# A bidirectional encoder layer on one core: PSUM banks kept through the Fourier stages, V in quarters, tables two tiles ahead, and h^T copies of odd blocks only

## The chip, the cores and the metric

The kernel runs on one core of a Trainium2 chip. The metric is the device time of one execution in microseconds, median of several runs. The core has TensorE (PE; its weight loads are listed as PEld), VectorE (DVE), ScalarE (ACT), GpSimd (POOL) and SyncE (SP), which here issues most of the DMAs. Work is in SBUF (128 partitions), matmuls add up in PSUM (eight banks), and the inputs and large intermediates lie in DRAM.

## The reference

16 learned meta tokens are put ahead of 2048 tokens of width 1024, and the stream (T = 2064 positions) passes a LayerNorm. One projection then feeds two mixers:

```python
def fourier_mix(u):
    ug = u.astype(jnp.float32).reshape(Bn, L, N_FOURIER_GROUPS, FOURIER_GROUP_DIM)
    y = jnp.fft.fft2(ug, axes=(1, 3), norm="ortho").real
...
proj = jnp.einsum("bld,de->ble", x, w_in)
u_f, qkv, beta_l, decay_l, z, gates = jnp.split(proj, cuts, axis=-1)
y_a = jnp.einsum("blf,fd->bld", fourier_mix(u_f), w_fourier_proj)
y_b = jnp.einsum("blf,fd->bld", gated_delta_branch(qkv, ...), w_delta_proj)
mix = jnp.einsum("bld,de->ble", gate_a * y_a + gate_b * y_b, w_out)
x = layer_norm(DEEPNORM_ALPHA * x + mix, ln1_g, ln1_b)
ff = jnp.einsum("blf,fd->bld", jnp.square(jax.nn.relu(jnp.einsum("bld,df->blf", x, w_up))), w_down)
```

The Fourier mixer takes the real part of a DFT over the 2064 positions and the 128 channels of each of four groups. The delta branch (short convolution on q, k, v; four heads; forward and backward scans), the gates, the output projection, the MLP and two more LayerNorms follow; the diff touches none of them. Inputs and output are fp32.

## The kernel before, in words

**Number format.** An fp32 operand is held as two fp16 halves, high and low. `split` (L56) makes them: ScalarE writes the high half, VectorE the rest. `mm3` (L91) then issues three matmuls for each block of 128 (high by high, high by low, low by high; L95 to L97).

**LayerNorm and channel DFT** (`phase_ln0_fourier`, L143). `ln(t)` loads a tile of 128 tokens (`x0`, three buffers), takes the statistics on VectorE with the root on GpSimd, normalises into `h`, stores `h` for later (`z_sc`), transposes it by TensorE into banks `ps0`, scales it on ScalarE into `ht` (four buffers), and splits it on VectorE into the fp16 halves `hb` (16 tiles of 128 tokens, four blocks of 512) and `hm` for the meta tokens. Each half of `ht` is also stored in fp32 to DRAM (`htd`, L194). `wprime(q)` (L203) multiplies the Fourier columns of the projection by the channel DFT table once, for eight q, and `uprime` (L196) multiplies h^T by that: `uT`, four row groups m of 128 channels by 2064 positions in fp32. Its eight weight loads `wt` are issued on ScalarE's queue (L165).

**Folding** (L232). The DFT over positions is made shorter by symmetry: for each m, positions are added to or subtracted from their mirror image twice (`f`, `f2`), transposed, and split into `V` (one tile of 128 x 2 halves x 2 parities x 5 blocks x 512 channels). All four m stand behind the last `uprime` in the program.

**Position DFT** (`phase_dft`, L255). Eight tables (sine or cosine s, parity, half of the frequencies c), each 0.5 MB in fp16, are loaded into `dtab` (three buffers), and for each two or three products of 15 matmuls are made into a bank `psf` and split into `yf` (m = 0, 1) or `y6`, the four channels in the middle of the groups. `y6` goes by three DMAs into `yf64`.

**ya** (`phase_ya`, L325). For each of eight column blocks d the weights are prepared (`prep_wf`, one d ahead), and in three steps of 344 positions the products for the even and the odd part are made, added and subtracted on VectorE into `ya`, and stored.

**Side work** (`h_ops`, L636). The later projections use a seven-product scheme (Strassen) and need sums of blocks of h^T: for each of two pairs of blocks and four column groups j, four blocks are loaded back from `htd` into `raw`, and T1 to T4 are made by four subtractions and split. `h_ops` is a generator: the stages resume it with `next(side)`, four times ahead of the DFT, once after each of its 16 large products, once after each of the 24 steps of ya; what is left runs at the end (`drive(side)`). Its instructions on ScalarE and VectorE are kept in program order.

**qkv** (`phase_qkv`, L713). It begins with `prep_in(0, ...)` (L810), which loads two blocks of the weights, makes four sums and seven split operands `wu` (eight buffers `tile16`) and stores these for the second pass. Then groups of seven products follow.

**What sets the order.** The program is written in this sequence, and a planner, which models each engine's time, gives each engine a fixed order: an instruction that is ready and stands earlier in the program goes first. Loads can so be issued long before their place, as soon as their buffer is free. On the chip each engine and each DMA queue keeps its order, and a waiting instruction holds back all behind it. A buffer pool that is opened later lies over the memory of pools that were closed, and its tiles wait until the tiles they lie on are no longer used: `winp` (`raw`, `sum`, `wu`), `yfp` (`yf`, `yf64`, `wfs`) and `dft` (`dtab`) lie over the tiles of the LayerNorm stage. The PSUM pools are separate for each stage: five banks `psf` and three `ps0` in LayerNorm, four `psf` in the DFT and ya.

Of the kernel before, what the change touches and what calls it, by code (L numbers as in the profile page):

```python
# [142 lines left out]
def phase_ln0_fourier(k, pr, vp):  # L143
# [8 lines left out]
    k.htd = k.dram.tile([4, 2, 4, P, 512], F32, name="htd")  # L152
    V = vp.tile([P, 2, 2, NQT, 512], F16, name="V")
    with k.pool("fft") as fp, k.pool("ln0") as lp, k.pool("ln0s") as sp, \
            k.pool("ln0p", bufs=3, space=PSUM) as tp, k.pool("fftp", bufs=5, space=PSUM) as pp:
# [8 lines left out]
        for q in range(KT):  # L164
            nc.scalar.dma_start(out=wt[:, q], in_=i["w_inf_t"][q])  # L165
# [3 lines left out]
        def ln(t):  # L169
# [9 lines left out]
            for q in range(2):  # L179
# [13 lines left out]
                if t > 0:  # L193
                    nc.sync.dma_start(out=k.htd[(t - 1) // 4, q, (t - 1) % 4].rearrange("p (j c) -> p j c", c=P), in_=ht)  # L194
# [8 lines left out]
        def wprime(q):  # L203
            wth = fp.tile([P, 2, 4, P], F16, name="wth", bufs=3)
            split(k, wth[:, 0], wth[:, 1], wt[:, q], S_W)
            ps = pp.tile([P, 4, P], F32, name="psf")
            for g in range(4):
                mm3(k, ps[:, g], lambda _: wth[:, 0, g], lambda _: wth[:, 1, g],
                    lambda _: ctab[:, 0], lambda _: ctab[:, 1], 1)
            pv = ps.rearrange("p g (s j) -> p g s j", s=2)  # L210
            dv = [wp[:, e, q].rearrange("p (s g j) -> p g s j", s=2, g=4) for e in range(2)]
            for e in range(2):
                split(k, dv[0][:, :, e], dv[1][:, :, e], pv[:, :, e], 1.0 / S_TAB)

        ln(0)
        ln(1)
        for q in range(KT):
            wprime(q)
        ln(2)
        for t in range(1, 5):  # L220
            if t == 1:
                uprime(range(4), 0, MT)
            uprime(range(4), MT + (t - 1) * P, P)
            for j in ((3,), (4,), (5, 6), (7, 8))[t - 1]:
                ln(j)
        for b in range(1, 4):
            for m in range(4):
                uprime([m], *HBLK[b])
                if b < 3:
                    ln(4 * b + 5 + m)  # L230
        for m in range(4):
# [7 lines left out]
            for par in range(2):  # L239
# [4 lines left out]
                for q in range(2):  # L244
# [5 lines left out]
                    o = [V[:r, e, par, 4 * q:4 * q + nb, m * P:(m + 1) * P] for e in range(2)]  # L250
                    split(k, o[0], o[1], ps[:r, :nb], 1.0)
    return V


def phase_dft(k, V, yp, fp, pp, side, h):  # L255

# [4 lines left out]
    y6 = fp.tile([4, 2, NK + 1], F16, name="y6")  # L261
    yf64 = yp.tile([68, NK + 1], F16, name="yf64")
    nc.gpsimd.memset(yf64, 0.0)
    for _ in range(4):
        next(side, None)
    wf0 = prep_wf(k, yp, 0, 1, h)
    for s in range(2):
        for par in range(2):
            for c in range(2):
                k0, kn = c * KW, min(KW, NQ - par - c * KW)  # L270
                tb = fp.tile([P, NQT, 2, KW], F16, name="dtab", bufs=3)
                src = i["dft_tab"][s, par, c]
                nc.sync.dma_start(out=tb[:, :4], in_=src[:4 * P].rearrange("(n p) e k -> p n e k", p=P))
                nc.sync.dma_start(out=tb[:rl, 4], in_=src[4 * P:])
                for m in range(3 - s):
                    M = P if m < 2 else 4
                    cols = slice((2 * s + m) * P, (2 * s + m + 1) * P) if m < 2 else slice(256, 512, 64)
                    ps = pp.tile([P, 512], F32, name="psf")
                    for n in range(NQT):
# [7 lines left out]
                    if m < 2:  # L287
                        next(side, None)
# [666 lines left out]
def drive(g):  # L955
    for _ in g:
        pass
# [924 lines left out]
```

## Time and profile before

| What | Value |
|---|---|
| median of 3 runs | 2747.83 us (2745.06 to 2750.65) |
| profiled execution | 2750.99 us, its span 2749.2 us, mean granted clock 0.982 |
| TensorE busy | 2614.9 us, 95% of the span |
| VectorE busy | 1944.4 us, 71% |
| ScalarE busy | 1210.4 us, 44% |
| DMA | 521.81 MB, mean 190 GB/s |
| first 280 us (stages that the diff touches) | about a tenth of the span |

A time in the trace is counted from the first instruction. "PE" rows are matmuls, which overlap, so that the distance from one start to the next says more than a duration. An arrow in brackets names who ended the idle time ahead of an instruction. The granted clock is TensorE's, 1.00 being full speed.

### The profile page before, as it was taken

How to read it: one execution, taken by the hardware profiler on the slowest of the kernel's cores; microseconds unless marked ns; L12 is line 12 of the kernel's file. 1: busy time of each engine (PE TensorE's matmuls, PEld its weight loads, DVE VectorE, ACT ScalarE, POOL GpSimd, SP SyncE). 2: the span in 40 equal slices, each digit the busy share in tenths (PEclk: the TensorE clock that was granted, in tenths of full speed). 3: DMA queues.
4: the chain of work that ended last, by engine and by line, in shares of the span. 5: the costliest groups of instructions: out<-in, count | busy, mean ns of one | idle time of the engine just before them, and what ended most of it. 6: DMA issues, size and time to landing. Idle time of an engine off the chain costs nothing.

```text
span 2749.2 us, 42069 instructions
## 1 busy us (share of the span) xinstructions
PE 2614.9 (95%) x15087; PEld 1393.4 (51%) x15087; DVE 1944.4 (71%) x3785; ACT 1210.4 (44%) x2772; POOL 401.6 (15%) x559
## 2 busy tenths in 40 slices
PE   6987999999899989999999999999999999999997
PEld 6454555455554449986444444444444444444443
DVE  7558897888878316687968688888888655545556
ACT  5434565555563325685222454444553422222232
POOL 1000131121010001263156500000001300000003
PEclk9988999999999999999999999999999999999999
DMA  7568666589898757774822674444446733333311
GB/s 263 190 204 289 208 222 209 165 285 305 283 322 287 268 193 227 219 243 143 282 86 76 191 284 141 144 152 161 169 169 242 244 100 104 100 104 100 103 43 73
DMA packets 325850, 521.81 MB, mean 190 GB/s; under 512 B 84220, under 2 KB 136396, under 8 KB 321672
## 3 DMA queue, kind: packets, MB, share of 16 engines
q1 hardware_dynamic: 320712, 512.88, 56.5%
q10 hardware_dynamic: 4928, 6.24, 0.7%
q8 instruction: 118, 1.93, 0.3%
q14 instruction: 92, 0.75, 0.1%
HBM read 311.30 MB, written 207.69 MB: 189 GB/s over the span
## 4 chain that ended last, share of the span: by engine, by line
PE 67%; DVE 15%; DMA 7%; issue 3%; ACT 3%; POOL 3%; SPq 1%; DVEq 0%; POOLq 0%; ACTq 0%
PE mm L95 17%; PE mm L97 17%; PE mm L96 17%; DVE wu L59 2%; PE psf L95 1%; PE psf L97 1%; PE psf L96 1%; PE psc L1216 1%; DVE hid L498 1%; PE psc L1241 1%; DVE hb L59 1%; PE psc L1233 1%; PE psc L1253 1%; PE psc L1224 1%; DVE acc L1578 1%
## 5 line engine op out<-in xcount | busy, mean ns | idle before, releaser
L95 PE MATMUL mm<-hb,wu 128*128 128x512 f16 x1280 | 487.8, 381 | 12.4 <-ACT wu L58 7.4
L96 PE MATMUL mm<-hb,wu 128*128 128x512 f16 x1280 | 487.5, 381 | 0.0
L97 PE MATMUL mm<-hb,wu 128*128 128x512 f16 x1280 | 487.3, 381 | 0.0
L1578 DVE TENSOR_TENSOR acc<-acc,mm 128x512 f32<-128x512 f32 x420 | 285.5, 683 | 150.2 <-PE mm L97 149.4
L95 PE MATMUL mm<-wdn,hid 128*128 128x512 f16 x904 | 342.2, 379 | 13.4 <-DVE acc L1578 13.3
L96 PE MATMUL mm<-wdn,hid 128*128 128x512 f16 x904 | 342.6, 379 | 0.0
L97 PE MATMUL mm<-wdn,hid 128*128 128x512 f16 x904 | 342.5, 379 | 0.2 <-DVE hid L498 0.2
L95 PEld LDWEIGHTS <-wu 128*128 128x128 f16 x1900 | 185.2, 98 | 220.1 <-ACT wu L58 11.8
L96 PEld LDWEIGHTS <-wu 128*128 128x128 f16 x1900 | 184.9, 98 | 218.2 <-issue 18.7
L97 PEld LDWEIGHTS <-wu 128*128 128x128 f16 x1900 | 184.6, 98 | 213.8 <-issue 5.4
L95 PE MATMUL mm<-ht,wu 128*128 128x512 f16 x512 | 196.7, 384 | 8.0 <-DVE c L606 4.2
L96 PE MATMUL mm<-ht,wu 128*128 128x512 f16 x512 | 196.6, 384 | 0.0
L97 PE MATMUL mm<-ht,wu 128*128 128x512 f16 x512 | 196.0, 383 | 0.0
L498 DVE TENSOR_TENSOR hid<-c,hid 128x512 f16<-128x512 f32 x158 | 107.3, 686 | 124.9 <-ACT hid L497 124.7
L66 POOL TENSOR_SCALAR ln_rs<-ln_mv 128x1 f32<-128x1 f32 (+1 forms) x49 | 13.7, 280 | 1192.4 <-DVE ln_mv L76 1182.5
L497 ACT CAST hid<-c 128x512 f16<-128x512 f32 x158 | 95.7, 614 | 183.7 <-PE mm L97 155.1
L96 PEld LDWEIGHTS <-hid 128*128 128x128 f16 x904 | 88.4, 98 | 122.7 <-issue 19.7
L751 DVE SCALAR_TENSOR_TENSOR conv<-rawc,cw,conv 128x512 f32<-128x512 f32 x192 | 135.0, 741 | 14.9 <-ACT conv L749 14.5
L58 ACT ACTIVATE wdn<-raw 128x512 f16<-128x512 f32 x78 | 46.4, 622 | 222.6 <-PE mm L97 187.3
L97 PEld LDWEIGHTS <-hid 128*128 128x128 f16 x904 | 88.3, 98 | 108.2 <-DVE hid L498 2.2
L95 PEld LDWEIGHTS <-hid 128*128 128x128 f16 x904 | 88.4, 98 | 107.2 <-ACT hid L497 1.2
L58 ACT ACTIVATE wu<-raw 128x512 f16<-128x512 f32 x145 | 88.0, 622 | 77.5 <-PE mm L97 45.2
(385 smaller groups left out, 4982.3 us busy)
## 6 DMA issues: line engine op xcount, KB each, us to landing
wu<-op SPq DMA_DIRECT2D x245, 256.0 KB
op<-wu SPq DMA_DIRECT2D x203, 256.0 KB
wdn<-op SPq DMA_DIRECT2D x112, 256.0 KB
op<-wdn SPq DMA_DIRECT2D x98, 256.0 KB
kq<-kqd SPq DMA_DIRECT2D x46, 512.0 KB
raw<-in_w_down SPq DMA_DIRECT2D x36, 512.0 KB
raw<-in_w_qz SPq DMA_DIRECT2D x32, 512.0 KB
gt<-c SPq DMA_DIRECT2D x64, 256.0 KB
```

The source lines that it names most:

```text
L58: nc.scalar.activation(out=hi, in_=src, func=AF.Copy, scale=scale)
L59: nc.vector.scalar_tensor_tensor(out=lo, in0=src, scalar=scale, in1=hi, op0=ALU.mult, op1=ALU.subtract)
L95: mm(ps, lhsT=whi(q), rhs=xhi(q), start=first and q == 0, stop=False, skip_group_check=skip)
L96: mm(ps, lhsT=whi(q), rhs=xlo(q), start=False, stop=False, skip_group_check=skip)
L97: mm(ps, lhsT=wlo(q), rhs=xhi(q), start=False, stop=last and q == nk - 1, skip_group_check=skip)
L497: k.nc.scalar.copy(t[:, 0], src)
L498: k.nc.vector.tensor_tensor(out=t[:, 1], in0=src, in1=t[:, 0], op=ALU.subtract)
L751: nc.vector.scalar_tensor_tensor(out=s, in0=src[:, j:j + m], scalar=cw[:, c, j:j + 1], in1=s, op0=ALU.mult, op1=ALU.add)
L1216: nc.tensor.matmul(ps[:, h], lhsT=kq[:, h, 0], rhs=S[:, h], start=True, stop=True)
L1224: nc.tensor.matmul(psq[:, h], lhsT=kq[:, h, 1], rhs=S[:, h], start=True, stop=True)
L1233: nc.tensor.matmul(psv[:, h], lhsT=T_[:, h], rhs=R[:, h], start=True, stop=True)
L1578: nc.vector.tensor_tensor(out=c, in0=c, in1=ps, op=ALU.add)
```

## The change

- The `psf` pool (five banks) is opened once, around LayerNorm, DFT and ya.
- `V` becomes four tiles, one for each m, and a small fifth one (`V6`) with the middle channels, filled by ScalarE copies. `fold(0)` and `fold(1)` stand behind the last `uprime` of m = 2 and m = 3, `fold(2)` and `fold(3)` at the end.
- The tables get two buffers in pool `dft` and one, `dtab0`, in the pool of V, which lies over nothing; each table is loaded two to three steps ahead. The third product of a step (middle channels) comes after the next step's two, and its results go straight into `yf64`.
- `h_ops` is resumed twice after each DFT product and no more ahead of them. `prep_wf` is two d ahead.
- `htd` is stored for the second and fourth block of h^T only; `h_ops` takes the others from the fp16 halves, with one VectorE instruction more for each of two sums.
- The first qkv operands are made by the same side generator, behind `h_ops`; the call at the start of `phase_qkv` goes.
- `wprime` writes its bank in the order of the result, so that one split does for two; seven of eight `wt` loads move to SyncE's queue.

```diff
-    k.htd = k.dram.tile([4, 2, 4, P, 512], F32, name="htd")
-    V = vp.tile([P, 2, 2, NQT, 512], F16, name="V")
+    k.htd = k.dram.tile([2, 2, 4, P, 512], F32, name="htd")
+    V = [vp.tile([P, 2, 2, NQT, P], F16, name="V%d" % m) for m in range(4)]
+    V.append(vp.tile([P, 2, 2, NQT, 4], F16, name="V6"))
...
-                if t > 0:
+                if t > 0 and (t - 1) // 4 % 2:
...
-            ps = pp.tile([P, 4, P], F32, name="psf")
+            ps = pp.tile([P, 512], F32, name="psf")
+            pv = ps.rearrange("p (s g j) -> p g s j", s=2, g=4)
...
-            for e in range(2):
-                split(k, dv[0][:, :, e], dv[1][:, :, e], pv[:, :, e], 1.0 / S_TAB)
+            split(k, wp[:, 0, q], wp[:, 1, q], ps, 1.0 / S_TAB)
...
+                    o = V[m][:r, :, par, 4 * q:4 * q + nb]
+                    split(k, o[:, 0], o[:, 1], ps[:r, :nb], 1.0)
+                    if m > 1:
+                        for e in range(2):
+                            nc.scalar.copy(V[4][:r, e, par, 4 * q:4 * q + nb, 2 * m - 4:2 * m - 2], o[:, e, :, ::64])
+
+        ln(0)
+        for q in range(1, 4):
+            nc.sync.dma_start(out=wt[:, q], in_=i["w_inf_t"][q])
+        ln(1)
+        for q in range(4, KT):
+            nc.sync.dma_start(out=wt[:, q], in_=i["w_inf_t"][q])
...
+                elif m > 1:
+                    fold(m - 2)
+        fold(2)
+        fold(3)
...
+    def load():
+        if len(tabs) < len(steps):
+            t = steps[len(tabs)]
+            tb = tabs[t] = (fp.tile([P, NQT, 2, KW], F16, name="dtab", bufs=2) if len(tabs) % 3 else
+                            vp.tile([P, NQT, 2, KW], F16, name="dtab0"))
...
+            split(k, yf64[:4, ks], yf64[32:36, ks], ps[:M, :kn], ysc)
+            nc.scalar.copy(yf64[64:68, ks], yf64[:4, ks])
+        if m < 2:
+            next(side, None)
+            next(side, None)
+
+    for _ in range(3):
+        load()
+    third = []
+    for t in steps:
+        s = t[0]
+        load()
+        for m in range(2):
+            prod(t, m)
+        if t == steps[0]:
+            wf0 = [prep_wf(k, yp, d, 1, h) for d in range(2)]
+        if third:
+            prod(third.pop(), 2)
         if s == 0:
+            third.append(t)
...
-        if d + 1 < KT:
-            ops.append(prep_wf(k, mp, d + 1, 2))
+        if d + 2 < KT:
+            ops.append(prep_wf(k, mp, d + 2, 2))
...
-            r = [h.raw() for _ in range(2)]
+            r = h.raw()
             for q in range(2):
-                for e in range(2):
-                    nc.sync.dma_start(out=r[q][:, 512 * e:512 * e + 512], in_=k.htd[2 * p + e, q, j])
+                nc.sync.dma_start(out=r[:, 512 * q:512 * q + 512], in_=k.htd[p, q, j])
...
-            add(t1, b12, b11)
+            add(z(t1), z(b12), b11[:, 0, :, c])
+            add(z(t1), z(t1), b11[:, 1, :, c])
...
-            add(t4, b21, t2)
+            add(z(t4), b21[:, 0, :, c], z(t2))
+            add(z(t4), z(t4), b21[:, 1, :, c], ALU.add)
...
-        h.prep_in(0, [col(f) for f in G[0]])
...
+                pp = cy.enter_context(k.pool("psfp", bufs=5, space=PSUM))
...
-                    side = h_ops(k, h)
-                    pp = cy.enter_context(k.pool("dftp", bufs=4, space=PSUM))
+                    side = chain(h_ops(k, h), h.prep_steps(0, (4, 0)))
```

`chain` runs one generator after the other. `prep_steps`, `w_steps` and `left_steps` are `prep_in`, `prep_w` and `left` with pauses between the operands.

147 lines of the change are left out of this document (76 added, 71 removed).

## The prediction

> **What bounds the kernel now.** I read the page first, then the stretches of the stages that the diff touches, then TensorE's and SyncE's rows in order of time, and last VectorE's groups. The page says that TensorE bounds the program as a whole:
>
> ```profile
> span 2749.2 us, 42069 instructions
> PE 2614.9 (95%) x15087; PEld 1393.4 (51%) x15087; DVE 1944.4 (71%) x3785; ACT 1210.4 (44%) x2772; POOL 401.6 (15%) x559
> ```
>
> All edits lie before the qkv stage, so the share of the whole says little. The stretches by stage (time, then each engine's busy time, the granted clock, DMA):
>
> ```profile
> core 0: us, PE busy (x) PEld busy (x) DVE busy (x) ACT busy (x) POOL busy (x), PEclk, DMA share, GB/s
> 30.00:142.00 112.00, 102.17 (x885) 65.00 (x882) 68.21 (x138) 50.68 (x137) 13.11 (x33) 0.97 0.56 205
> 142.00:160.00 18.00, 9.42 (x46) 6.04 (x45) 15.43 (x34) 7.75 (x20) 0.96 (x1) 0.63 0.42 124
> 160.00:199.00 39.00, 38.97 (x298) 25.57 (x297) 20.91 (x40) 14.35 (x32) 0.00 (x0) 0.95 0.80 261
> 199.00:264.00 65.00, 52.71 (x312) 31.20 (x310) 52.78 (x110) 26.12 (x55) 0.34 (x1) 0.92 0.86 284
> 220.00:240.00 20.00, 14.76 (x93) 8.73 (x92) 19.79 (x41) 9.09 (x19) 0.00 (x0) 0.97 0.88 322
> 264.00:278.00 14.00, 5.07 (x26) 1.93 (x26) 7.92 (x19) 4.70 (x8) 0.00 (x0) 0.70 0.90 308
> ```
>
> They are: LayerNorm with the channel products (to 142), folding and transposes into V (to 160), the position DFT (to 199), ya (to 264), the entry of qkv (to 278). TensorE is full in the DFT, where VectorE is only half used (20.91 of 39). In ya VectorE is used to 81% (52.78 of 65), for a while to 99% (19.79 of 20), and TensorE waits. Around the two seams TensorE stands still and its clock falls. Its rows there (start, duration, in brackets the idle time and its releaser):
>
> ```profile
> 63.92 0.66 PE L182 MATMUL ps<-ident,h 128*128 128x128 f32 x4 [4.52 <-ACT ht L189]
> ...
> 142.02 1.15 PE L249 MATMUL ps<-ident,x 128*128 128x128 f32 x9
> ...
> 159.18 0.38 PE L95 MATMUL psf<-dtab,V 128*128 128x259 f16 x1 [4.47 <-DMA dtab<-in_dft_tab]
> 159.35 0.42 PE L96 MATMUL psf<-dtab,V 128*128 128x259 f16 x1
> 159.56 0.43 PE L97 MATMUL psf<-dtab,V 128*128 128x259 f16 x1
> ...
> 164.17 0.27 PE L95 MATMUL psf<-dtab,V 128*128 128x259 f16 x1
> 164.28 0.28 PE L96 MATMUL psf<-dtab,V 128*128 128x259 f16 x1
> ...
> 261.45 0.31 PE L95 MATMUL psf<-yf,wpm 128*128 128x344 f16 x1
> 261.60 0.31 PE L96 MATMUL psf<-yf,wpm 128*128 128x344 f16 x1
> ...
> 269.91 0.61 PE L95 MATMUL mm<-hb,wu 128*128 128x512 f16 x1 [7.42 <-ACT wu L58]
> 270.31 0.63 PE L96 MATMUL mm<-hb,wu 128*128 128x512 f16 x1
> ...
> 277.48 0.61 PE L95 MATMUL mm<-ht,wu 128*128 128x512 f16 x1 [3.02 <-ACT wu L58]
> ```
>
> The first seam runs from 142.02 to 159.18 us, the second from the end of ya (269.91 - 7.42 = 262.5) until qkv flows after 277.48. Matmuls follow each other at 0.11 us (259 columns) and 0.15 us (344) when warm, and at twice that right behind the idle time (159.35 to 159.56).
>
> SyncE's queue at the first seam shows what the tables wait for:
>
> ```profile
> 144.17 1.74 SPq L689 DMA_DIRECT2D raw<-htd  x4
> 153.32 1.42 SPq L298 DMA_DIRECT2D wfs<-in_wf_parts  x3
> 154.78 0.47 SPq L273 DMA_DIRECT2D dtab<-in_dft_tab  x1
> ```
>
> The raw blocks go out when uT is last read, wfs when the last fold is over, and the table behind them.
>
> **LayerNorm stage.** Half of the htd stores go, and seven of the eight wt loads move from ScalarE's queue to SyncE's, three ahead of the first full x tile. The wp split becomes one pair of instructions instead of two.
>
> VectorE's wait for x up to 290 us, and the transfers from 30 to 100 us:
>
> ```profile
> DVE ln_st L74 <- DMA x<-in_x: 9.3, 6, 2.0
> ...
> DMA packets 6450, 19.59 MB, mean 280 GB/s; under 512 B 704, under 2 KB 704, under 8 KB 6080
> ...
> htd<-ht SPq DMA_DIRECT2D x23, 256.0 KB
> ```
>
> VectorE's two groups of the folded weights, and the first of their loads:
>
> ```profile
> L59 DVE SCALAR_TENSOR_TENSOR wp<-psf,wp 128x256 f16<-128x256 f32 x16 | 6.1, 419 | 0.7 <-ACT wp L58 0.4
> L59 DVE SCALAR_TENSOR_TENSOR wth<-wt,wth 128x512 f16<-128x512 f32 x8 | 5.3, 684 | 0.2
> ...
> 1.74 0.94 ACTq L165 DMA_DIRECT2D wt<-in_w_inf_t  x2
> ```
>
> VectorE waits 9.3 us for x. From 30 to 100 us the engines move 19.59 MB at 280 GB/s, and 23 htd stores of 0.26 MB are 6 MB of it; half of them is 3 MB, or 10.7 us of transfer, at the place where x is late. The most that can come back is TensorE's idle time from 30 to 142, 112 - 102.2 = 9.8 us, and the slow clock, 3% of 112 = 3.4: 13 us. The wp split saves 6.1 - 5.3 = 0.8 us of VectorE. The other end: a wt load takes 0.94 / 2 = 0.47 us to issue, and seven of them put 3.3 us in front of x on SyncE: +3 us. I take -7, a little over the middle, because x is the wait that ends last there and its competitor is halved.
>
> The Trainium skill says in "DMA: Bandwidth & Descriptors", section "Issuing engines are not separate DMA queues", that all issuing engines feed the same 16 DMA engines and another issuer saves only the issuing time. It speaks against the move to SyncE: by it the transfers gain nothing and only the +3 us end is left of that edit; the -7 would be -4.
>
> **VectorE from the last fold to the end of the first qkv operands.** The groups of VectorE from 142.8 to 264 (count, busy us, mean ns):
>
> ```profile
> L59 DVE SCALAR_TENSOR_TENSOR V<-ps,V 128x512 f16<-128x512 f32 (+1 forms) x16 | 6.9, 478 | 1.6 <-ACT V L58 1.5
> L683 DVE TENSOR_TENSOR sum<-raw 128x512 f32<-128x512 f32 x15 | 10.2, 680 | 0.0
> L683 DVE TENSOR_TENSOR sum<-raw,sum 128x512 f32<-128x512 f32 x14 | 9.6, 686 | 0.2
> L59 DVE SCALAR_TENSOR_TENSOR yf<-psf,yf 128x259 f16<-128x259 f32 (+2 forms) x16 | 7.2, 450 | 13.7 <-ACT yf L58 13.7
> ```
>
> And three of its rows in order of time:
>
> ```profile
> 142.85 1.29 DVE L238 SCALAR_TENSOR_TENSOR h<-uT,sgn 128x1031 f32<-128x1031 f32 x1 [3.67 <-ACT uT L201]
> ...
> 266.79 0.68 DVE L683 TENSOR_TENSOR sum<-raw 128x512 f32<-128x512 f32 x1
> 267.39 0.68 DVE L673 TENSOR_TENSOR wu<-sum,wu 128x512 f16<-128x512 f32 x1
> ```
>
> The first is the last fold's beginning. The others give the pitch: such instructions take 0.68 us but follow each other at 0.60. I count in that pitch, as the stretches do.
> - Now: 15.43 + 20.91 + 52.78 = 89.1 us in the stretches, and behind 264 what is left of h_ops, eight instructions of which the two sum rows lack three of 32 adds, at 0.60, 4.8 us: 94.
> - Away: the V splits of block 0 move ahead of 142, a quarter of 6.9: -1.7.
> - New: each of the eight blocks of h_ops rebuilds b11 and b21 from two halves with two further adds: 16 x 0.60 = 9.6. The trace has no add of this mix (fp32 and fp16 in, fp32 out). Below, the plain fp16 cast of equal size at 0.42, above, the fp32 adds here; I take the upper end, since these are adds with an fp32 output. The lower would save 3 us.
> - Moved: the first qkv operands, four adds and seven splits, 11 x 0.60 = 6.6, from behind 276 into ya.
>
> Sum: 93.9 - 1.7 + 9.6 + 6.6 = 108.4 us. TensorE has 300 matmuls at 0.11 and 312 at 0.15 (the counts in the DFT and ya stretches) and some 30 transposes at 0.13: 33 + 46 + 4 = 83. **VectorE becomes the bound of this stretch.** That is the center of the forecast: the seams of TensorE vanish only as far as VectorE lets them.
>
> How well can it be used? The side work is called twice after each DFT product (32 calls) and once after each ya step (24): 56, which is what eight blocks of six calls, one call more and seven of operand work need; today there are 44, and what is left of them stands in the second seam. So the 18 us that VectorE idles in the DFT are filled. Bounds: 81% as in ya now, 98.9% as from 220 to 240. I take 88%, nearer to the first, because the splits still alternate with ScalarE (13.7 us of waits in the yf row). 108.4 / 0.88 = 123; from 142.85 to 266. TensorE can start qkv four instructions earlier, 4 x 0.60 = 2.4 us, at 263, with the last operands still being split.
>
> And now? The first product of qkv has 12 matmuls, done by 277.48, where the second begins cold again: 0.40 us apart (269.91 to 270.31), of which half is the warm rate. Taking as many cold matmuls behind 277.48 as the first product has, the 12 x 0.2 us lost there cancel the 12 x 0.2 us of work already done: as if qkv had begun warm at 277.5. Gain 277.5 - 263 = 14, less one for a clock that will not be full at the entry: **-13**, with bounds 277.5 - (142.9 + 108.4 / 0.989 - 2.4) = 27 and 277.5 - (142.9 + 108.4 / 0.81 - 2.4) = 3.
>
> **At nothing.** The tables two tiles ahead and the kept banks: their 4.47 us wait lies in the seam already counted, covered by VectorE's folds until about 153; without that cover it is 4.5 us. Three transfers y6 to yf64 become splits at the same price and four copies on ScalarE, idle for half of the DFT (14.35 of 39). Sixteen tiny V6 copies, at most 0.3 us each, fall on ScalarE in the folds (7.75 of 18). The second wf set made early: the same instructions, moved. The seven stores of the operands move into ya, where half of the htd loads fall away.
>
> **Sum.** -7 - 13 = -20 against the profiled execution's 2750.99: 2731. The median of the runs is 3.2 lower, 2747.83, so **2728 us**. The stages behind 278 should move forward as they are: their order does not depend on a fixed time.
>
> **Rivals.**
> - *VectorE full, LayerNorm's waits all gone* (-27 - 13 = -40: 2708). For it: 19.79 of 20. Against: a stretch of 110 us with four engines in turns.
> - *VectorE no better used than in ya today* (-3, and LayerNorm -1: 2744). For it: the adds are new work on the engine that becomes the bound. Against: the wf operands, which caused part of ya's waits, come one step earlier.
> - *The tables do not come early*, because their two other buffers lie over tiles of LayerNorm that the folds use to the end: wfs goes out at 153.3 for that reason. Then the second table lands at 158, TensorE has had two products of the DFT, and VectorE lost some yf splits that it makes up for: +3, 2731.
> - *Slower: TensorE's clock.* TensorE would have 83 us of work in 120 and be idle in between for VectorE. Behind idle time the rows show half rate. If the granted clock stays low over the whole stretch, TensorE takes over as the bound once its mean is below 83 / 120 = 0.69. At half rate the work takes 166 us, to 309 instead of 277.5: +31 - 7 = +24, on the scale of the median 2772. For it: 0.63 and 0.70 at the seams. Against: 0.97 from 220 to 240, where TensorE is busy 14.76 of 20, much as it would be.
>
> The Trainium skill, "TensorE: Matmul & The Clock Gate", section "Part 1: The HAM clock gate (the "warmup" mystery)", has this as a rule: an idle window of about 3.4 us halves the clock, and as much busy time frees it. The trace agrees with the halving (0.22 against 0.11 us); the waits of the stretch from 220 to 240 stayed below what brings it about.
>
> **How the numbers follow.** Forecast 56% (2716 to 2737: LayerNorm -10 to -3, VectorE used to 95 or 85%), full use 12%, poor use 17%, late tables 9%, clock 6%. What a measurement here can tell from no change is 0.2%, some 5.5 us, so from 2742.3 to 2753.3 is the same. Faster: nearly all of the forecast, full use, late tables and a little of poor use: 0.79. Same: most of poor use: 0.12. Slower: clock and the tail of poor use: 0.09. The range leaves out the clock and the far half of full use: 2709 to 2747.
>
> **What would show it.** VectorE busy above 85% between the last fold and qkv, with TensorE idle in small pieces and a clock above 0.9; the first DFT product within 3 us of the last channel product; no wait of TensorE over 3 us for wu at the entry of qkv, and that entry near 257; the idle time before 63.92 shorter. It is wrong if TensorE still waits for whole tables, if qkv begins later than 272, or if qkv begins early and the gain is lost behind it.

## The result and the profile after

| | before | after |
|---|---|---|
| median beside the prediction | 2749.24 us (2741.34 to 2752.35, 8 runs) | 2733.27 us (2723.02 to 2737.39, 8 runs) |
| ratio | | 0.9941, 95% interval 0.9924 to 0.9958 |
| same two kernels, repeated with the first experiments | 2752.15 us (11 runs) | 2731.11 us (6 runs), 0.9921, 0.9906 to 0.9935 |
| profiled execution | 2750.99 us, span 2749.2, clock 0.982 | 2723.02 us, span 2721.2, clock 0.988 |

The forecast was 2728, from 2709 to 2747. The change gains 16 to 21 us. The two profiles differ by 28, more than the medians, because the profiled execution after is the quickest of its eight; an experiment below deals with that. One execution of the kernel copies_one below took 5465.8 us, twice the others, for a cause that isn't known, and is left out of its median. The page after says:

```profile
PE 2604.6 (96%) x15087; PEld 1394.3 (51%) x15087; DVE 1950.3 (72%) x3793; ACT 1212.5 (45%) x2784; POOL 402.0 (15%) x559
```

The stretches of the changed kernel, cut at nearly the places that the prediction used for the one before (time, busy time of each engine, granted clock, DMA):

```profile
core 0: us, PE busy (x) PEld busy (x) DVE busy (x) ACT busy (x) POOL busy (x), PEclk, DMA share, GB/s
30.00:142.00 112.00, 101.22 (x768) 63.65 (x765) 68.94 (x139) 52.62 (x140) 13.81 (x33) 0.95 0.56 198
142.00:160.00 18.00, 17.27 (x138) 11.53 (x136) 16.19 (x37) 11.72 (x40) 0.96 (x1) 1.00 0.52 151
160.00:199.00 39.00, 32.08 (x213) 20.04 (x212) 34.16 (x65) 18.17 (x38) 0.00 (x0) 0.87 0.81 257
199.00:220.00 21.00, 17.45 (x115) 11.05 (x114) 20.48 (x42) 9.44 (x20) 0.00 (x0) 1.00 0.88 310
220.00:240.00 20.00, 15.75 (x104) 9.91 (x104) 19.83 (x43) 9.28 (x19) 0.00 (x0) 1.00 0.87 324
240.00:264.00 24.00, 24.00 (x151) 12.89 (x150) 19.32 (x47) 11.83 (x24) 2.71 (x4) 1.00 0.87 302
264.00:278.00 14.00, 14.00 (x87) 6.68 (x86) 13.77 (x22) 7.89 (x16) 0.87 (x2) 1.00 0.57 194
```

The first stretch is nearly as it was. From 142 to 160 TensorE is busy 17.27 of 18 us instead of 9.42, from 264 to 278 14 of 14 instead of 5.07: both seams are gone. In between VectorE is nearly full (19.83 of 20, 20.48 of 21), and TensorE now has its idle pieces there. TensorE's rows at the same landmarks:

```profile
58.92 1.05 PE L182 MATMUL ps<-ident,h 128*128 128x128 f32 x4 [3.45 <-ACT ht L189]
...
139.87 1.15 PE L231 MATMUL ps<-ident,x 128*128 128x128 f32 x9
140.85 0.27 PE L95 MATMUL psf<-dtab,V 128*128 128x259 f16 x1
140.96 0.28 PE L96 MATMUL psf<-dtab,V 128*128 128x259 f16 x1
...
194.72 0.31 PE L96 MATMUL psf<-yf,wu 128*128 128x344 f16 x1 [3.37 <-DVE yf L59]
...
249.57 0.38 PE L95 MATMUL mm<-hb,wu 128*128 128x512 f16 x1
249.78 0.38 PE L96 MATMUL mm<-hb,wu 128*128 128x512 f16 x1
```

The first DFT product starts at 140.85 instead of 159.18, at the warm pitch of 0.11 us and without idle time ahead of it. The qkv products begin at 249.57 without a wait and at 0.21 us apart, instead of 269.91 and 0.40. SyncE's queue shows what moved:

```profile
14.53 0.78 SPq L283 DMA_DIRECT2D dtab<-in_dft_tab  x1
...
120.96 0.38 SPq L283 DMA_DIRECT2D dtab<-in_dft_tab  x1
...
200.21 0.94 SPq L734 DMA_DIRECT2D raw<-htd  x2
201.20 0.42 SPq L579 DMA_DIRECT2D raw<-in_w_qz  x1
```

The first table goes out at 14.5 and the next two at 121 (before, the first at 154.78). Before, the loads of raw and wfs stood ahead of the first table in this queue, and SyncE waited 21.6 us for raw's buffer and 7.4 us for that of wfs, both held by the folds. Now the three tables stand ahead of raw (142.02) and wfs (147.59). The last copy of h^T goes out at 200; before, two such loads still stood at the end of ya:

```profile
257.70 2.16 SPq L689 DMA_DIRECT2D raw<-htd  x1
...
261.59 0.42 SPq L689 DMA_DIRECT2D raw<-htd  x1
```

A landmark that all kernels here have, and which I call the entry of qkv, is the transposes of the first and of the last qkv result. In the changed kernel, by the view of that line (count, shortest, median and longest duration in ns, first to last start):

```profile
L815 PE MATMUL pst<-ident,conv x196: 272/273/394, 298.4 to 523.3; 128*128 128x128 f32 x192, 128*16 128x128 f32 x4
L815 PE MATMUL pst<-ident,kqm x4: 272/272/273, 294.5 to 383.9; 128*16 128x128 f32 x4
```

Before, they stand at 319.4 (first) and 546.2 (last). So the entry of qkv moved by 24.9 us, of which 2.2 were gained up to the end of the channel products (142.82 to 140.67, the end of the last uT on ScalarE). The landmark lies some 45 us behind the first qkv product. That product moved by 20.3 us (269.91 to 249.57); the rest was gained behind it, where TensorE, before the change, waited once more (3.02 us ahead of 277.48) and ran at the cold pitch. Between the two also lies a wait of TensorE for lg on ScalarE, outside of the edited stages:

```profile
286.39 3.49 PE L422 MATMUL psb<-wb,hb 128*128 128x32 f16 x128 [2.69 <-ACT lg L427]
```

### The profile page after: what moved, and what is told of

It is laid out like the page before. It is cut to its first block, busy times and chain, and to the rows that moved or that the text cites. A ratio compares the mean times of both kernels' runs of the same rounds, so it can differ in the third digit from the quotient of the medians.

```text
span 2721.2 us, 42002 instructions
## 1 busy us (share of the span) xinstructions
PE 2604.6 (96%) x15087; PEld 1394.3 (51%) x15087; DVE 1950.3 (72%) x3793; ACT 1212.5 (45%) x2784; POOL 402.0 (15%) x559
## 4 chain that ended last, share of the span: by engine, by line
PE 67%; DVE 12%; DMA 6%; POOL 4%; ACT 3%; issue 3%; SPq 1%; DVEq 0%; POOLq 0%; ACTq 0%
PE mm L95 17%; PE mm L97 17%; PE mm L96 17%; DVE wu L59 1%; PE psc L1264 1%; PE psc L1289 1%; PE psc L1281 1%; PE psc L1301 1%; DVE hid L529 1%; PE psc L1272 1%; PE psf L95 1%; PE psm L95 1%; POOL hr L1412 1%; PE psm L97 1%; PE psm L96 1%
## 5 line engine op out<-in xcount | busy, mean ns | idle before, releaser
L95 PE MATMUL mm<-wdn,hid 128*128 128x512 f16 x904 | 342.1, 379 | 13.4 <-DVE acc L1626 13.3
L95 PE MATMUL mm<-ht,wu 128*128 128x512 f16 x512 | 194.6, 380 | 5.5 <-DVE c L652 3.4
L96 PE MATMUL mm<-ht,wu 128*128 128x512 f16 x512 | 194.5, 380 | 0.0
L97 PE MATMUL mm<-ht,wu 128*128 128x512 f16 x512 | 194.3, 380 | 0.0
```

Of the source, the lines that this page charges most:

```text
L95: mm(ps, lhsT=whi(q), rhs=xhi(q), start=first and q == 0, stop=False, skip_group_check=skip)
L96: mm(ps, lhsT=whi(q), rhs=xlo(q), start=False, stop=False, skip_group_check=skip)
L97: mm(ps, lhsT=wlo(q), rhs=xhi(q), start=False, stop=last and q == nk - 1, skip_group_check=skip)
```

## The experiments

All kernels start from the changed one. "Ratio" is to the kernel before; "product" is the start of the first qkv product, "first" and "last" are the transposes above; "last copy" is when the last load of a copy of h^T begins to be issued. Each ratio is to executions of the kernel before that were taken beside it (medians 2750.1 to 2752.4).

| kernel | median us | ratio (95%) | last uT ends | last copy | product | first | last |
|---|---|---|---|---|---|---|---|
| before | | 1 | 142.8 | 261.6 | 269.9 | 319.4 | 546.2 |
| four_undone | 2743.7 | 0.9964 (0.9950 to 0.9979) | 142.2 | 250.9 | 261.4 | 306.3 | 536.1 |
| copies_one | 2739.6 | 0.9956 (0.9939 to 0.9973) | 141.3 | 249.3 | 260.3 | 304.9 | 534.6 |
| all_copies | 2736.8 | 0.9943 (0.9929 to 0.9958) | 141.6 | 228.6 | 257.6 | 301.5 | 530.1 |
| one_next | 2732.9 | 0.9928 (0.9908 to 0.9948) | 139.0 | 213.6 | 252.8 | 297.7 | 527.4 |
| tabs_late | 2731.0 | 0.9918 (0.9897 to 0.9938) | 140.3 | 201.6 | 251.7 | 295.6 | 525.6 |
| wt_scalar | 2731.0 | 0.9925 (0.9901 to 0.9949) | 142.6 | 200.2 | 249.7 | 294.0 | 524.6 |
| again (unaltered) | 2731.1 | 0.9921 (0.9906 to 0.9935) | 139.9 | 198.1 | 247.8 | 293.5 | 522.7 |
| qkv_late | 2726.9 | 0.9905 (0.9891 to 0.9920) | 140.6 | 198.7 | 248.0 | 292.3 | 520.9 |
| wf_banks | 2725.0 | 0.9912 (0.9896 to 0.9929) | 139.2 | 195.5 | 247.4 | 292.0 | 521.2 |
| gp_adds | 2728.6 | 0.9915 (0.9896 to 0.9933) | 139.7 | 215.3 | 247.9 | 289.2 | 518.9 |
| no_low_adds | 2724.5 | 0.9897 (0.9880 to 0.9913) | 139.3 | 211.2 | 245.3 | 288.1 | 517.8 |
| gp_x4 | 2724.5 | 0.9906 (0.9891 to 0.9921) | 138.8 | 214.3 | 246.5 | 287.8 | 516.2 |

The entry of qkv in the profiles tells more than the medians, which differ by less than their spread in the lower half of the table. But the changed kernel itself, in its two profiles, differs by 1.8 us at the first qkv product (249.57 and 247.79) and by 1.0 at the first transposes: a step of that size isn't told apart.

**The kernel once more.** No edit.

> The changed kernel once more, unaltered. The pair of profiles differs by 28 us and the medians by 16. If the profile shown was simply a quick execution, this one's profile is at 2730 to 2737, with the channel products ending at 140 and the first transposes of the qkv results at 294 to 296 as there, and the difference lies behind 300. If the entry of qkv itself varies from execution to execution, the transposes move by more than 3 us.

The landmarks repeat within 1 us (139.9, 293.5, 522.7), and this profile's execution is 12 us longer at the end, as expected. The difference lies behind the qkv stage, in stretches that the change doesn't touch. The stretch from 525 to 900 us, first in the profile after, then in this one:

```profile
525.00:900.00 375.00, 354.48 (x1826) 189.91 (x1825) 298.35 (x848) 190.09 (x394) 39.19 (x139) 0.99 0.89 298
```

```profile
525.00:900.00 375.00, 355.06 (x1789) 191.85 (x1788) 294.41 (x841) 186.21 (x386) 38.49 (x139) 0.97 0.87 290
```

The granted clock is 0.97 instead of 0.99, and fewer instructions are done in the same time. From the last transpose to the end of the span the thirteen profiles of changed kernels need 2197 to 2211 us, 2204.8 on average, and the one before 2203.0. So 28 us was the quick execution, and the change's own gain is 24.9 us at the entry of qkv and 22.9 to 23.5 at its end.

**First qkv operands made at the entry of qkv.**

```
-                    side = chain(h_ops(k, h), h.prep_steps(0, (4, 0)))
+                    side = h_ops(k, h)
 ...                                          # in phase_qkv
+        h.prep_in(0, [col(f) for f in G[0]])
```

> The changed kernel with the first qkv operands made at the entry of qkv again. Theory, that part brought the second seam by letting qkv products run into the end of ya: without it TensorE stands idle for 8 to 12 us before qkv and starts cold, the first transposes of qkv results move from 294.5 to 305 to 311, and the whole is 10 to 16 us slower than the changed kernel. Rival, VectorE's work only moves from one place to another: the 6.6 us come off ya's end, and the whole is 0 to 4 us slower.

Both are wrong: the entry is not later, but 1 to 2 us earlier, and the whole 4 us faster, about what the medians can tell. The load of the first weights on SyncE in this kernel:

```profile
198.72 0.95 SPq L734 DMA_DIRECT2D raw<-htd  x2
199.71 0.43 SPq L579 DMA_DIRECT2D raw<-in_w_qz  x1
```

It stands where it stood (201.20 in the changed kernel), and the operands are still made between ya's additions. The plan takes the operands forward as soon as the sums of h^T are done, wherever the program has them. What held qkv back in the kernel before was not where its operands stood in the program but that the sums of h^T were late: one_next and copies_one, below, bring the seam back by late sums alone.

**Copies of all four blocks.**

```
-    k.htd = k.dram.tile([2, 2, 4, P, 512], F32, name="htd")
+    k.htd = k.dram.tile([4, 2, 4, P, 512], F32, name="htd")
-                if t > 0 and (t - 1) // 4 % 2:
+                if t > 0:
 ...                                          # in h_ops, as before the change
+            b11, b12, b21, b22 = r[0][:, :512], r[0][:, 512:], r[1][:, :512], r[1][:, 512:]
+            add(t1, b12, b11)
+            add(t4, b21, t2)
```

> The changed kernel with fp32 copies of all four blocks again: 3 MB more stores in the LayerNorm stage, 4 MB more loads behind it, and 16 adds fewer on VectorE. If the halved copies bring LayerNorm what I forecast of them (most of 7 us), the channel products end 3 to 6 us later than 140, VectorE's 9.6 us come back behind it, and the whole is the same within 4 us as the changed kernel. Rival, the transfers were hidden: the channel products end within 1 us of 140, and the whole is 5 to 9 us faster than the changed kernel.

Neither. LayerNorm loses only 0.9 to 1.6 us (141.6 against 139.9 and 140.7), but the entry of qkv is 7 to 8 us later and the whole 5.7 us slower, although VectorE has 16 adds less to do: the last copy is loaded at 228.6 instead of 200. The stretch from 195 to 250, in this kernel and then in the changed one:

```profile
195.00:250.00 55.00, 39.65 (x224) 22.95 (x223) 47.42 (x97) 22.88 (x49) 0.00 (x0) 0.84 0.92 308
```

```profile
195.00:250.00 55.00, 46.87 (x318) 29.39 (x315) 54.24 (x113) 24.86 (x52) 0.34 (x1) 0.97 0.86 315
```

With all copies VectorE is less busy, the DMA engines more (0.92), and TensorE does 7 us less at a lower clock. The kernel no_low_adds, below, has as many VectorE operations as this one but the halved copies: its entry is 13.4 us earlier (288.1; 12.4 at the first qkv product), and that is what the halved copies bring. Whether the volume or SyncE's queue holds the loads back wasn't separated. The raw tiles alone aren't it: the kernel with the adds on GpSimd also takes two of them for each block and has its entry at 289.

**Side work resumed once after each product; and this together with all copies.**

```
         if m < 2:
             next(side, None)
-            next(side, None)
```

> The changed kernel with the side work resumed once after each product of the position DFT, as before, so 16 times fewer ahead of the end of ya. Theory, the second seam stood where the sums of h^T were not done when ya ended: they are late again, the last load of an fp32 copy goes out after 230 (now about 200), the first transposes of qkv results move from 294 to 303 to 312, and the whole is 8 to 16 us slower than the changed kernel. Rival, the plan pulls the sums forward whatever the program resumes: the transposes within 2 us of 294, the whole within 3 us.

> The changed kernel with fp32 copies of all four blocks and with the side work resumed once after each product of the DFT: two parts undone at once. Alone, the copies moved the first transposes of qkv from 294 to 301.5 and the single resume to 297.7. Theory, the two cover for each other, since either brings the last load of a copy back from 261 (before) to 229 or 214: together that load goes out after 240 and the transposes move to 310 to 319, the whole to 12 to 20 us above the changed kernel. Rival, they add: transposes at 304 to 306, the whole 7 to 11 us above.

One resume alone costs 3 to 4 us at the entry, less than I expected and more than the rival. But the second seam is back: the last ya add starts at 240.22, some 8 to 10 us earlier than in the changed kernel (248.41 and 250.19), and then TensorE waits 14.23 us for a sum of the first operands, and starts cold. The side work that no longer stood ahead of ya's adds stands behind them; the early end of ya pays for most of the wait. Both together give 304.9, the sum of the two (294 + 7.5 + 3.7): they do not cover for each other. TensorE's row in one_next, then in copies_one:

```profile
252.80 0.61 PE L95 MATMUL mm<-hb,wu 128*128 128x512 f16 x1 [14.23 <-DVE sum L550]
```

```profile
260.30 0.61 PE L95 MATMUL mm<-hb,wu 128*128 128x512 f16 x1 [18.07 <-DVE sum L549]
```

**16 adds less.**

```
-            add(z(t1), z(t1), b11[:, 1, :, c])
...
-            add(z(t4), z(t4), b21[:, 1, :, c], ALU.add)
```

> The changed kernel without the 16 adds of the low halves of b11 and b21 (T1 and T4 then lack those halves: the computation is changed in that part, the time is read for 16 adds less). Theory, VectorE is the bound from the last fold to qkv (93% busy there): 16 x 0.60 = 9.6 us leave it, the last ya add comes 5 to 9.6 us earlier than 250, and the whole is 5 to 9 us below the changed kernel. Rival, TensorE and the order of the plan set the end there: 0 to 2 us.

The entry comes 5.4 to 6.4 us earlier, the whole is 6.6 us below the repeated kernel. At the end of the stretch itself less is seen: the last ya add comes 2.3 to 4.0 us earlier (246.14), short of the 5 to 9.6 expected, and the first qkv product 2.5 to 4.3 (245.25). Some of the rest is the wait for lg behind it (1.4 us instead of 2.7 and 2.9). TensorE's waits for ya's adds from 140 to 300 us (sum, count, longest) fall to

```profile
PE psf L95 <- DVE ya L386: 2.3, 3, 1.1
```

from, in the changed kernel,

```profile
PE psf L95 <- DVE ya L386: 7.1, 6, 1.7
```

So VectorE is the bound of the stretch for a part: of 9.6 us taken away 2.5 to 4 show up at its end. A wait of TensorE for a table (2.9 us for dtab) is new.

**These adds on GpSimd.** It puts b11 and b21 together from their halves into a raw tile; VectorE keeps four operations for each block.

```
+            for f, b in ((f11, b11), (f21, b21)):
+                nc.gpsimd.tensor_tensor(out=z(f), in0=b[:, 0, :, c], in1=b[:, 1, :, c], op=ALU.add)
...
+            add(t1, b12, f11)
+            add(t4, f21, t2)
```

> The changed kernel with b11 and b21 put together from their halves by GpSimd (16 adds into raw tiles), and on VectorE the four fp32 operations of before for each block: 16 adds fewer on VectorE, the loads still halved. GpSimd took 0.35 us for 128 x 88 in fp16, so by size about 2 us for each of these, 33 us in a stretch in which it is idle. Theory, VectorE is the bound: the transposes of qkv 4 to 7 us earlier than 294, and the whole 4 to 7 us below the changed kernel. Rival, GpSimd's work comes late or slows VectorE down (its adds above 0.75 us each): no gain, or up to 6 us slower.

The entry is 4.3 to 5.3 us earlier, but the stretch itself ends no earlier: the last ya add starts at 248.76 and the first qkv product at 247.87, where the repeated kernel has 248.41 and 247.79. What differs lies behind: TensorE no longer waits 2.7 to 2.9 us for lg. The whole is 2.5 us below the repeated kernel, which the medians don't resolve. GpSimd's group and one row of it, then VectorE's rows at that time:

```profile
L741 POOL TENSOR_TENSOR raw<-hb 128x512 f32<-128x512 f16 x16 | 24.8, 1570 | 34.9 <-DVE sum L729 34.9
...
168.79 3.09 POOL L741 TENSOR_TENSOR raw<-hb 128x512 f32<-128x512 f16 x2 [7.51 <-DVE sum L729]
```

```profile
168.63 0.68 DVE L719 TENSOR_TENSOR ht<-sum,ht 128x512 f16<-128x512 f32 x1
169.23 1.64 DVE L729 TENSOR_TENSOR sum<-raw 128x512 f32<-128x512 f32 x1
170.79 1.64 DVE L719 TENSOR_TENSOR ht<-sum,ht 128x512 f16<-128x512 f32 x1
```

While GpSimd adds, a VectorE instruction takes 1.64 us instead of 0.68. What the adds free is lost again: from 140 to 248.7 VectorE needs as long for 190 instructions here as for 206 in the repeated kernel.

```profile
140.00:248.70 108.70, 92.25 (x662) 59.22 (x660) 102.51 (x190) 55.07 (x129) 26.05 (x18) 0.97 0.77 258
```

```profile
140.00:248.70 108.70, 93.95 (x665) 60.33 (x664) 102.30 (x206) 54.74 (x129) 1.30 (x2) 0.95 0.79 267
```

**Late tables.**

```
-            tb = tabs[t] = (fp.tile(..., name="dtab", bufs=2) if len(tabs) % 3 else
-                            vp.tile(..., name="dtab0"))
+            tb = tabs[t] = fp.tile([P, NQT, 2, KW], F16, name="dtab", bufs=3)
```

> The changed kernel with all three DFT tables in the pool that lies over the LayerNorm tiles, none loaded early. Theory, the early table and the warm clock behind it brought the first seam: the first DFT product starts 3 to 6 us after the last channel product (now 1.0) with the clock below 0.9 there, and the transposes of qkv come 2 to 5 us later than 294. Rival, VectorE sets the end of the stretch and makes up for it: the first product late as above, the transposes within 1.5 us of 294, the whole within 3 us of the changed kernel.

It is nearer to the rival: the first product starts 7.6 us later, at 148.46 and cold, and the entry only 1 to 2 us later (2 to 4 at the first qkv product). Most of the delay is made up for within the stretch.

```profile
148.46 0.43 PE L95 MATMUL psf<-dtab,V 128*128 128x259 f16 x1
```

But the edit did less than its name says: the three tables were still issued at 120 to 123, far ahead of the 154.78 of before, and the transfers were over by 127. The first product didn't wait for its table. It stands behind the last fold's transposes in the order that the plan gave TensorE (147.37, then 148.46 without a wait), where the changed kernel has it between them.

**Four parts undone at once:** all copies, one resume, this table pool, operands at the entry.

> Copies of all blocks, the single resume, late tables and the first qkv operands at the entry: four parts undone at once. With the first two undone the transposes of qkv stood at 304.9; before they stood at 319.4. Late tables alone cost 1.6 and late operands nothing, while VectorE was the bound; with the sums late (last load of a copy at 249) it isn't. Theory, these two are worth something only then: the first DFT product at 148, the transposes at 312 to 320, the whole at 2745 to 2753. Rival, they stay worth little, and the missing 14.5 us lie in what is still in place (folds between the channel products, V in quarters, the transfers of the third product): the transposes at 304 to 308, the whole at 2738 to 2744.

The rival holds: 306.3, 1.4 us behind copies_one. 13 us to the kernel before remain, in what is still in place. SyncE's and TensorE's rows show one difference:

```profile
122.26 0.39 SPq L282 DMA_DIRECT2D dtab<-in_dft_tab  x1
...
150.07 0.43 PE L95 MATMUL psf<-dtab,V 128*128 128x259 f16 x1
```

The tables go out 32 us earlier than before and the DFT begins 9.1 us earlier (159.18 before). The rows divide these 9.1: 4.5 are the wait for the first table, which is gone, and the other 4.6 are transposes of the folds that end earlier (the last group starts at 148.98, before at 153.40). The tables' pool is as before and their order in SyncE's queue isn't (they stand ahead of raw at 143.51 and wfs at 148.90), which points to the order of the loads. But it isn't shown that the early start reaches the entry: copies_one has its first product at 141.43, 8.6 us earlier still, and its entry is only 1.4 us earlier. Nearer to the entry, ya's last add starts at 246.25 instead of 263.50 and the last copy at 250.9 instead of 261.6. Which edits bring that wasn't separated, so the 13 us stay unassigned.

**Weights of ya one block ahead, and separate PSUM pools.**

```
-            wf0 = [prep_wf(k, yp, d, 1, h) for d in range(2)]
+            wf0 = [prep_wf(k, yp, 0, 1, h)]
...
-        if d + 2 < KT:
-            ops.append(prep_wf(k, mp, d + 2, 2))
+        if d + 1 < KT:
+            ops.append(prep_wf(k, mp, d + 1, 2))
...
-                pp = cy.enter_context(k.pool("psfp", bufs=5, space=PSUM))
+                    with k.pool("fftp", bufs=5, space=PSUM) as pl:
+                    pp = cy.enter_context(k.pool("dftp", bufs=4, space=PSUM))
```

> The changed kernel with the weights of ya prepared one block ahead instead of two and with PSUM pools separate for LayerNorm and the DFT: two parts that I priced at nothing. If they cost nothing, the transposes of qkv stay within 1.5 us of 294 and the whole within 3 us of the changed kernel. Rival, the waits of TensorE for wpm (7.7 us before, none in the changed kernel) and for the first bank come back: the transposes at 298 to 303, the whole 4 to 8 us slower.

Nothing is lost: the entry is 1.5 to 2.5 us earlier, and the wait for wpm doesn't come back. The median is 6 us lower than the repeated kernel's, but the kernel before was 2 us quicker beside it too, and the intervals of the two ratios overlap.

**wt loads on ScalarE's queue.**

```
-        nc.scalar.dma_start(out=wt[:, 0], in_=i["w_inf_t"][0])
+        for q in range(KT):
+            nc.scalar.dma_start(out=wt[:, q], in_=i["w_inf_t"][q])
```

> The changed kernel with the eight wt loads on ScalarE's queue again. Theory, LayerNorm is bound by the chain of x, statistics and ht, which the early start of the channel products only turned into waits: the first channel product on hb starts at about 31 instead of 20.5, the waits between 45 and 70 shrink by as much, and the channel products end at 139 to 142 as now. Rival, the earlier start is what LayerNorm gained: they end 5 to 10 us later than 140 and the whole is slower by as much.

The first theory holds but for its size: the channel products start 12 us later (at 32.1 instead of 20.0), end 2 to 2.7 us later (142.6, a little past the range), and the entry of qkv is where it was, within what the two unaltered profiles differ by. ScalarE's queue issues until 13 us; behind it stand five us of ht and then the first split of wth, at 18.05 instead of 5.55:

```profile
3.18 7.55 ACTq L166 DMA_DIRECT2D wt<-in_w_inf_t  x6
12.86 0.34 ACTq L167 DMA_DIRECT2D sgn<-in_fold_sgn  x1
```

**Four x tiles**, with the adds on GpSimd: `name="x0", bufs=3` becomes `bufs=4` in both places.

> The changed kernel with the halves of b11 and b21 added on GpSimd, as run before, and four buffers for the x tiles of LayerNorm instead of three. Theory, x comes late for want of a buffer: VectorE's wait for x falls from 6 to below 2 us, the channel products end at 134 to 138 instead of 140, the transposes of qkv at 284 to 288 (289 with the GpSimd adds alone), the whole 6 to 11 us below the changed kernel. Rival, LayerNorm is bound by the chain behind x or by the transfers: the products end within 1 us of 140, the whole as with the GpSimd adds alone (0 to 5 us below the changed kernel).

By the mechanism it is the rival. VectorE's wait for x falls only from 6.3 to

```profile
DVE ln_st L74 <- DMA x<-in_x: 5.2, 5, 2.2
```

and the channel products end 0.9 us earlier than in gp_adds, at 138.8. The entry (287.8) and the whole (6.6 us below the repeated kernel) fall at the near end of the theory's ranges, but only 1.4 us of the entry came with the fourth tile. What TensorE waits for in LayerNorm is ht and hb (in the changed kernel 10.6 us from 30 to 142); both come from x by way of the statistics, so this doesn't yet say which link of that chain is the slow one:

```profile
PE ps L182 <- ACT ht L189: 4.8, 4, 3.5
PE psf L95 <- DVE hb L191: 4.3, 2, 2.6
PE psf L96 <- DVE hb L192: 1.5, 2, 0.9
```

No kernel here is surely faster than the changed one: the intervals of all their ratios overlap with that of the repeated kernel. Those with the lowest ratios that compute the same are the one with operands at the entry, the one with four x tiles and the one with separate banks.

## Why the prediction was right, and where its steps were wrong

The number came out 3 to 5 us low (2728 against 2731 and 2733), since two terms were off in opposite directions (LayerNorm gained less, the entry of qkv more) and a part of the gain isn't seen at the end. That the number is so near is in part luck: a term of 13 came out as 22.7 and one of 7 as 2 to 3.

- **LayerNorm stage, -7.** Mis-sized, for a wrong reason: it gained 2.2 to 2.9. I took x for the wait that ends last and the halved copies for its competitor. The copies are worth 0.9 to 1.6 us, a further x buffer 0.9. TensorE's waits are for ht and hb; what makes these late stays open.
- **The bad end of the wt move, +3.** Wrong in sign. The move brings 2 to 2.7 us: ScalarE's first split starts at 5.55 instead of 18.05, since it neither issues the loads ahead of it nor has ht ahead of it in the plan. The Trainium skill ("DMA: Bandwidth & Descriptors", "Issuing engines are not separate DMA queues") says that another issuer saves only the issuing time; here it was ScalarE's issuing time that counted, since its computing stands in the same queue.
- **"VectorE becomes the bound of this stretch."** Right in the main. From 139.9 to 250.2 it is busy 102.2 of 110.3 us. Taking 16 adds away moves the end of the stretch by 2.5 to 4 of 9.6 us, so it is not the bound throughout. A late first DFT product and a late LayerNorm, 7.6 and 2 us, reach the entry as 1 to 2 and 0.
- **108.4 us at 88%.** Both were off, and by my own formula that is the rest: 102.2 / 0.93 = 110 us instead of 123. Of the 6 us of work four operand instructions of eleven, 2.4 us, stand behind ya's end, and two more of the folds' rows (1.3 us) had moved ahead of 139.9 with the splits; the rest wasn't traced. The use was 93%, where I had leaned to ya's 81%. The price of an add on fp16 and fp32 was right at its upper end:

```profile
L729 DVE TENSOR_TENSOR sum<-sum,hb 128x512 f32<-128x512 f32 x16 | 10.9, 684 | 0.0
...
L729 DVE TENSOR_TENSOR sum<-raw,hb 128x512 f32<-128x512 f32 x8 | 5.5, 684 | 0.0
```

- **"TensorE can start qkv four instructions earlier", -13 in all.** Too small: the gain from the last fold to qkv was 24.9 - 2.2 = 22.7. TensorE doesn't wait for ya's end: qkv products need one operand at a time, and the plan sets them right behind ya's last product (249.57, while ya's last add is at 250.19), so the stage begins warm. Of the 22.7, 4.6 lie behind the first qkv product, where the second wait and the cold pitch went.
- **56 resumes, two after each product.** Right that they fill VectorE's idle time and remove the seam: with one resume it stands there again, 14.23 us. But at the entry this is worth only 3 to 4 us, since the same work, done ahead of ya, delays ya's end by 8 to 10.
- **"At nothing": the tables two ahead and the kept banks.** Right for the banks and for ya's weights (292.0 without them). Wrong for the tables as a reading of the seam: I let VectorE's folds cover them until 153. But the first product needs only a quarter of V and its table, and started at 140.85 with the last fold still under way. Alone the table pool costs 1 to 2 us at the entry. What loads at 155, as before, would cost wasn't run.
- **"Where half of the htd loads fall away"**, said in passing and priced at nothing: the largest single term, 7 to 8 us net of the adds, 13.4 without them.
- **"The stages behind 278 should move forward as they are."** Nearly: qkv itself gives back 2.0 to 2.4 us (24.9 to 22.9, 25.9 to 23.5). Behind it the profiles vary by 13 us with the clock, which is more than what is left between 23 at the end of qkv and 16 to 21 in the medians. Whether something is lost there stays open.

Of the signs that I named, VectorE above 85%, the clock above 0.9 (0.95), the first DFT product within 3 us (1.0) and no wait for wu at the entry were seen; that entry, by the first qkv product, came at 250, not 257.

The rivals: poor use didn't come. VectorE's use came out between the forecast and full use (93% between 88 and 98.9), without LayerNorm's gain. The late tables didn't come either, and the reason given for them doesn't hold: in tabs_late and four_undone all three tables lie in the pool over the LayerNorm tiles and still go out at 120 to 125, long before the folds end.

The clock fell in pieces but didn't stay low: 0.87 on average from 160 to 199 (0.75 from 170 to 180), 1.00 from 199 to 278. The prediction took an idle window of about 3.4 us as what halves the clock, and held that the waits from 220 to 240 stayed below it. Neither fits the rows. In the kernel before, a wait of 3.67 us lies in that stretch, and by 240.08 the matmuls follow each other at 0.29 us instead of 0.15. In the changed kernel a wait of 2.55 us was enough: behind it they follow each other at 0.22 us instead of 0.11, until 181.7.

```profile
238.29 0.32 PE L95 MATMUL psf<-yf,wpm 128*128 128x344 f16 x1 [3.67 <-ACT wpm L58]
...
240.08 0.49 PE L96 MATMUL psf<-yf,wpm 128*128 128x344 f16 x1
```

```profile
175.91 0.37 PE L95 MATMUL psf<-dtab,V 128*128 128x258 f16 x1 [2.55 <-DVE yf L59]
176.08 0.42 PE L96 MATMUL psf<-dtab,V 128*128 128x258 f16 x1
176.30 0.42 PE L97 MATMUL psf<-dtab,V 128*128 128x258 f16 x1
```

So the clock did cost something (half rate from 176.1 to 181.7, and once more from 195.7 to 198.8), but it never became the bound of the stretch.

## What to carry to other kernels

When several edits feed one stretch, find its bound first and price each edit as "what it takes off the bound": here a first DFT product 7.6 us late and a stage before it 2 us late cost 1 to 2 and 0 us at the entry of qkv, while 16 adds on the fullest engine cost 5 to 6 there. Measure at more than one landmark: of these only 2.5 to 4 lay in the stretch, and the adds on GpSimd, 4 to 5 us better at the later landmark, gained nothing at the nearer one. A load that is halved shortens more than its own stage: follow its data to the last one that waits for them, here the sums whose lateness held qkv back. Where a planner orders the work, moving a piece in the program may change nothing; removing what it waits for does.

## What was not expected of the hardware

GpSimd's adds of 128 x 512 in fp16 take 1.57 us on average, and VectorE's instructions beside them 1.64 instead of 0.68 us (168.79 to 172.4). The Trainium skill, "SBUF — State Buffer", section "Who interferes with whom", says that a VectorE instruction with two SBUF inputs and a GpSimd instruction that reads SBUF share one port and block each other; the rows agree. So 16 adds moved there freed 16 x 0.60 = 9.6 us and cost VectorE back, in the sum and ht rows alone, (0.915 - 0.685) x 16 + (0.839 - 0.686) x 16 = 6.1 us:

```profile
L729 DVE TENSOR_TENSOR sum<-raw 128x512 f32<-128x512 f32 x16 | 14.6, 915 | 0.9 <-DMA raw<-htd 0.8
L719 DVE TENSOR_TENSOR ht<-sum,ht 128x512 f16<-128x512 f32 x16 | 13.4, 839 | 0.0
```

With the wu rows (0.723 instead of 0.686) and what isn't counted here, VectorE's busy time came out as it was (102.5 against 102.3 us up to 248.7). The entry is 4 to 5 us earlier all the same, for something behind the stretch: TensorE's wait for lg is gone there. What changed the order there stays open.
